# Routing ahead of expert 0, zeros under the scattered sums, and another order of the last experts

## The chip, the cores and the metric

The kernel runs on one core of a Trainium2 chip. A time is device microseconds of one execution, and the figure that counts is the median of a few executions on the same chip. TensorE (PE, with PEld for its weight loads), VectorE (DVE), ScalarE (ACT) and GpSimd (POOL) each work through their own instructions in order; SyncE (SP) does little else than issue transfers. POOL issues some transfers too.

## What is computed

One decoder layer for 512 tokens of width 1024: a token mixer (two kinds of attention, gated and projected), a layer norm, then a mixture of 32 experts of which each token takes 4, and a second layer norm. Cut to what matters here:

```python
x = layer_norm(ALPHA * x + token_mixer(x), ln1_g, ln1_b)          # y below
logits = x @ router_w + router_b
top_val, top_idx = top_k(logits, 4); gates = softmax(top_val)
# for each expert e, over the tokens that chose it:
#   g = min(x @ w_gate[e] + b_gate[e], 7); u = clip(x @ w_up[e] + b_up[e], -7, 7)
#   ffn[token] += gate * ((g * sigmoid(1.702 * g) * (u + 1)) @ w_down[e] + b_down[e])
out = layer_norm(ALPHA * x + ffn, ln2_g, ln2_b)                     # ALPHA = 2 ** 0.25
```

All is float32. One expert's three weight matrices are 12 MiB, all of them 384 MiB, and every expert's weights are read once.

## The kernel before, in words

**Front.** x and the projection weights are loaded in 1 MiB chunks through a ring of SBUF tiles, split into a high and a low part by ACT and DVE, and multiplied on PE. The very first chunk comes in four pieces, each with its two rows of x (`first_chunk`). Attention, gates and output projection follow. At the end of this part `norm_tile(t)` makes the normed rows y of 128 tokens (t = 0 to 3) in the tiles `r_tiles[t]`, POOL stores them to `y_dram`, PE turns them into `yT`, and after every second tile `route_places` multiplies them with the router's weights (PE, tile `pl`), takes the top 4 and gives each token its place in its experts' lists (`pos1`). ACT computes the norm's square root there, and later the exponentials of the softmax; between the two it loads another function table.

**Experts.** Two fixed experts (0 and 1) come first; the other 30 are ranked by their token counts on the chip (`rank_experts`), and the list `TURNS` says which rank is taken when. The first 18 in rank have two blocks of slots, A and B ("big"), the others one block ("small"). `slots` finds an expert's tokens with DVE compares and small PE products, and POOL gathers their rows from `y_dram` (tile `xg`). `ffn` then runs the expert: the rows are turned (`ptx`, `tx`), `pga` (and `pgb` for block B) collect gate and up, DVE and ACT make the hidden rows (`up`), PE turns them (`pth`, `th`), `pda` (and `pdb`) collect the result, ACT scales it by the routing weights (`sw`) to `ys`, and POOL adds those rows to `acc_dram` by a scattering transfer. `midway()` is code that stands between gate/up and down of expert i and prepares expert i + 2. In expert 0 it first calls `first_weights`: the ranking, the softmax weights (`route_weights`, result `gat`), the weights' split for experts 0 and 1 (`info`) and their products on PE (`late_weights`, tile `pw`), then ALPHA times y on ACT and four stores of it to `acc_dram`, with which the sums begin. Then the tiles of y are released, and two more ring tiles (`ring_d`) take their place.

**Weights.** SP issues the 384 chunks of expert weights in order into rings of 21 chunk tiles in all. A chunk's transfer waits until the chunk 21 before it has been used by PE (for a big expert by its block B too), and from expert 2 on the address needs the ranking (`order_i`).

**End.** `load_sums` reads the four tiles of `acc_dram`, the last expert's rows are added by a product with a 0/1 matrix (`psf`, read by DVE at L1014), and the second norm follows, tile by tile. A branch that would take further blocks of overfull experts stands between the loads and that product.

The order of the instructions on each engine is set by a scheduler from the program's dependences and priorities; only what follows `issue_after` is held behind a named instruction.

Of the kernel before, what the change touches and what calls it, by code (L numbers as in the profile page):

```python
# [19 lines left out]
P = 128  # L20
S = 512
# [15 lines left out]
def _turns():  # L37

    big, small = list(range(FIXED, BIG)), list(range(BIG, NE))
    turns, n, early = list(range(FIXED)), NE - FIXED - 1, NE - BIG - 1  # L40
    for i in range(n):
        some = small if len(small) > 1 and (NE - BIG - len(small)) * n <= i * early + n // 2 + 2 else big
        turns.append(some.pop(0))
    return turns + small


TURNS = _turns()
# [10 lines left out]
def decoder_kernel(tc, d):  # L58
# [3 lines left out]
    def mm(out, lhsT, rhs, start, stop, pos=None):  # L62
        if pos is None:
            T.matmul(out, lhsT, rhs, start=start, stop=stop)  # L64
        else:
            T.matmul(out, lhsT, rhs, start=start, stop=stop, tile_position=pos)  # L66
# [67 lines left out]
    ps = psO.tile([P, S], F32, name="ps_warm", tag="o")  # L134
    for n in range(8):
        mm(ps, warm[:, :P], warm, True, True)

    oT_h = [p_out.tile([P, S], F32R, name=f"oTh{c}") for c in range(10)]
    oT_l = [p_out.tile([P, S], F32R, name=f"oTl{c}") for c in range(10)]
# [370 lines left out]

    ring_c = tc.alloc_tile_pool(name="ring_c", bufs=RING[3], side="right")
    rings.append(ring_c)
    dpool = tc.alloc_tile_pool(name="dp", bufs=1, space=DRAM)
    y_dram = dpool.tile([S + P, D], F32, name="y_dram")
    acc_dram = dpool.tile([S + P, D], F32, name="acc_dram")

    mo1 = tc.alloc_tile_pool(name="mo1", bufs=1, side="right")
    p_y = tc.alloc_tile_pool(name="p_y", bufs=1, side="right")
    p_ln = tc.alloc_tile_pool(name="p_ln", bufs=1, side="left")
# [55 lines left out]
    def norm_tile(t):  # L575

        y = r_tiles[t]
        yT = yT_tiles[t % 2]
        sums = p_ln.tile([P, 2], F32, name=f"sums{t}", tag="sums", bufs=2)
        with tc.high_priority():  # L580
            for n in range(2):
                cs = slice(n * 512, (n + 1) * 512)
                V.scalar_tensor_tensor(y[:, cs], y[:, cs], ALPHA, mix[t][n], op0=ALU.mult, op1=ALU.add,
                                       accum_out=sums[:, n:n + 1])
            sq = yT[0].rearrange("p k c -> p (k c)").bitcast(BF16)
            nmu, rs = norm_stats(y, sums, sq, p_ln, f"a{t}")
        for n in range(2):
            cs = slice(n * 512, (n + 1) * 512)
            V.scalar_tensor_tensor(y[:, cs], y[:, cs], nmu, g1[:, cs], op0=ALU.add, op1=ALU.mult)
        for n in range(2):  # L590
            cs = slice(n * 512, (n + 1) * 512)
            V.scalar_tensor_tensor(y[:, cs], y[:, cs], rs, b1[:, cs], op0=ALU.mult, op1=ALU.add)
        G.dma_start(y_dram[t * P:(t + 1) * P, :], y)
        if t == 0:
            G.dma_start(y_dram[S:, :], y)
        for n in range(2):
            pt = psT.tile([P, S], F32, name=f"yTp{t}{n}", tag="t")
            for k in range(4):
                T.transpose(pt[:, k * P:(k + 1) * P], y[:, (4 * n + k) * P:(4 * n + k + 1) * P], ident)
            last["yT"] = A.copy(yT[n], pt.rearrange("p (k c) -> p k c", k=4))  # L600
        return yT
# [10 lines left out]
        V.tensor_tensor(oh, C[:, None, None, C_IOTA:C_IOTA + NE].broadcast_to([P, 2, 4, NE]),  # L612
                        if8[:, :, 0:4, None].broadcast_to([P, 2, 4, NE]), op=ALU.is_equal)

    def route_places(tp, yTs):

        t0 = 2 * tp
        pl = psA.tile([P, S], F32, name=f"pl{tp}", tag="acc")
        for tt in range(2):
            for k in range(KT):  # L620
                mm(pl[:, tt * NE:(tt + 1) * NE], yTs[tt][k // 4][:, k % 4, :], rw[:, k, :], k == 0, k == KT - 1)
        lg = small([2, NE], "lg", tp, pool=p_ln)
        V.tensor_tensor(lg, pl[:, :2 * NE].rearrange("p (t e) -> p t e", t=2),
                        rb[:, None, :].broadcast_to([P, 2, NE]), op=ALU.add)
        v8, i8, if8 = small([2, 8], "v8", tp), small([2, 8], "i8", tp, U32), small([2, 8], "if8", tp)
        for tt in range(2):
            V.max(v8[:, tt, :], lg[:, tt, :])
            V.max_index(i8[:, tt, :], v8[:, tt, :], lg[:, tt, :])
        V.tensor_copy(if8, i8)
        oh = small([2, 4, NE], "oh", tp, pool=p_ln)  # L630
        choose(oh, if8)
        mask = small([2, NE], "mask", tp, pool=p_ln)
        V.tensor_reduce(mask, oh.rearrange("p t k e -> p t e k"), axis=AX.X, op=ALU.add)
        V.tensor_copy(maskb[:, t0:t0 + 2, :], mask)
        pp = psA.tile([P, S], F32, name=f"pp{tp}", tag="acc")
        for tt in range(2):
            for u in range(t0 + tt + 1):
                mm(pp[:, tt * NE:(tt + 1) * NE], ubf if u == t0 + tt else obf, maskb[:, u, :], u == 0, u == t0 + tt)
        last["place"] = V.scalar_tensor_tensor(
            pos1[:, t0:t0 + 2, :], pp[:, :2 * NE].rearrange("p (t e) -> p t e", t=2), 1.0, mask,  # L640
            op0=ALU.add, op1=ALU.mult)
        return v8, if8

    def route_weights(tp, v8, if8):

        t0 = 2 * tp
        nmx, se, g4 = small([2], "nmx", tp), small([2], "se", tp), small([2, 4], "g4", tp)
        oh = scratch(f"weights{tp}", 8 * NE).rearrange("p (t k e) -> p t k e", t=2, k=4)
        choose(oh, if8)
        V.tensor_scalar(nmx, v8[:, :, 0], -1.0, None, op0=ALU.mult)  # L650
        for tt in range(2):
            A.activation(g4[:, tt, :], v8[:, tt, 0:4], AF.Exp, bias=nmx[:, tt:tt + 1], accum_out=se[:, tt:tt + 1])
        V.reciprocal(se, se)
        V.tensor_tensor(g4, g4, se[:, :, None].broadcast_to([P, 2, 4]), op=ALU.mult)
        V.tensor_tensor(oh, oh, g4[:, :, :, None].broadcast_to([P, 2, 4, NE]), op=ALU.mult)
        V.tensor_reduce(gat[:, t0:t0 + 2, :], oh.rearrange("p t k e -> p t e k"), axis=AX.X, op=ALU.add)
# [23 lines left out]
    for t in range(NT):  # L680
        mix_step(t, 4, first)
    late += w_out_splits(3)
    yTs, picks = [], []
    for t in range(NT):
        for n in range(2):
            for k in range(5, KT):
                mix_step(t, k, late[k - 5], (n,))
        yTs.append(norm_tile(t))
        if t % 2:
            picks.append(route_places(t // 2, yTs[-2:]))  # L690
    pc = psA.tile([P, S], F32, name="pc", tag="acc")
    for t in range(NT):
        mm(pc[:, :NE], obf, maskb[:, t, :], t == 0, t == NT - 1)
# [195 lines left out]
        V.tensor_reduce(order, table, axis=AX.X, op=ALU.add)  # L889
        V.tensor_copy(order_i, order[0:1])  # L890

    def first_weights():
        rank_experts()
        for tp in range(2):
            route_weights(tp, *picks[tp])
        for e in range(FIXED):
            sws[e] = late_weights(e, states[e], info_of(e, gat[:, :, e], mo1), psX, "t")
        for t in range(NT):
            A.mul(r_tiles[t], r_tiles[t], ALPHA)
            G.dma_start(acc_dram[t * P:(t + 1) * P, :], r_tiles[t])  # L900
        p_y.release()
        rings.append(tc.alloc_tile_pool(name="ring_d", bufs=RING[4], side="right", reuse_waits="tile"))

    def expert(i):
        def midway():
            if i == 0:
                first_weights()
            if i + 2 < NE:
                r = TURNS[i + 2]
                one = mo1.tile([P, NE], F32, name=f"one{i + 2}", tag="one", bufs=2)  # L910
                V.tensor_scalar(one, rank, float(r), None, op0=ALU.is_equal)
                place, weight = picked_columns(i + 2, one)
                states[i + 2], sws[i + 2] = all_slots(i + 2, 2 if r < BIG else 1, place[:, :, None],
                                                      order[:96, r:r + 1], weight, psX, "t")

        def next_rows():
            if i + 1 < NE:
                xts[i + 1] = rows_of_x(states[i + 1], i + 1)

        if i < FIXED:  # L920
            src = d["w_exp"][i]
        else:
            er = nc.values_load(order_i[:, TURNS[i]:TURNS[i] + 1], engines=[mybir.EngineType.SP], min_val=0,
                                max_val=NE - 1)
            src = d["w_exp"][bass.ds(er, 1)][0]
        return ffn(i, lambda c: load_expert(src[c], f"we{i}_{c}_"), states[i], lambda: sws[i], xts.pop(i), midway,
                   next_rows)
# [4 lines left out]
        add_rows(expert(i), states[i])  # L932

    ys_last, = expert(NE - 1)
    free = free_tiles(4)
    goes = free[0][:, :S]
    to = mo.tile([P, 1], F32, name="to")
    to_t = mo.tile([P, NT], F32, name="to_t")
# [5 lines left out]
    ln2 = free[1].rearrange("p (n c) -> p n c", n=2)  # L944
    nc.sync.dma_start(ln2[:, 0, :], d["ln2_g"].partition_broadcast(P))
    nc.sync.dma_start(ln2[:, 1, :], d["ln2_b"].partition_broadcast(P))
    sums = [t.rearrange("p (n c) -> p n c", n=2) for t in free[2:]]
    r_last = [sums[t // 2][:, t % 2, :] for t in range(NT)]

    def load_sums():  # L950
        for t in range(NT):
            nc.sync.dma_start(r_last[t], acc_dram[t * P:(t + 1) * P, :])

    load_sums()


# [172 lines left out]
```

## Time and profile before

| | |
|---|---|
| three runs | 1579.11, 1581.71, 1582.24 us (median 1581.71) |
| profiled execution | 1580.91 us, its span 1579.0 us |
| PE busy | 1472.5 us, 93% of the span |
| DVE, ACT, POOL busy | 463.5, 323.8, 154.4 us |
| moved by transfers | 475.27 MB, mean 301 GB/s |

The span is cut into 40 slices of about 39.5 us in the page's second part; each digit is the busy share of an engine, or of the 16 transfer engines, in tenths. A timeline row gives start, length, engine, line, operation, out<-in, how many instructions are merged in it, and in brackets how long the engine stood idle before it and what ended that. A row of waits gives a total, how many times, and the longest.

### The profile page before, as it was taken

How to read it: one execution, taken by the hardware profiler on the slowest of the kernel's cores; microseconds unless marked ns; L12 is line 12 of the kernel's file. 1: busy time of each engine (PE TensorE's matmuls, PEld its weight loads, DVE VectorE, ACT ScalarE, POOL GpSimd, SP SyncE). 2: the span in 40 equal slices, each digit the busy share in tenths (PEclk: the TensorE clock that was granted, in tenths of full speed). 3: DMA queues.
4: the chain of work that ended last, by engine and by line, in shares of the span. 5: the costliest groups of instructions: out<-in, count | busy, mean ns of one | idle time of the engine just before them, and what ended most of it. 6: DMA issues, size and time to landing. Idle time of an engine off the chain costs nothing. (4 is left out here: it accounts for less than half of the span.)

```text
span 1579.0 us, 24838 instructions
## 1 busy us (share of the span) xinstructions
PE 1472.5 (93%) x10022; PEld 794.1 (50%) x10022; DVE 463.5 (29%) x1344; ACT 323.8 (21%) x699; POOL 154.4 (10%) x121
## 2 busy tenths in 40 slices
PE   9999999999997799999998989988989998988993
PEld 6988767788885244353433335332433343332431
DVE  3134577764434331211221112111211111210114
ACT  4233466533323001011101001100101000100003
POOL 0000000000001011111111111111111010111102
PEclk9999999999996889999999999999999999999996
DMA  6202111333487399999999999999999999999992
GB/s 257 78 30 73 35 44 39 139 108 103 164 329 290 141 354 402 411 407 403 407 410 403 411 409 409 407 404 410 406 412 402 408 405 406 409 409 401 411 384 109
DMA packets 84758, 475.27 MB, mean 301 GB/s; under 512 B 10272, under 2 KB 12832, under 8 KB 39200
## 3 DMA queue, kind: packets, MB, share of 16 engines
q1 hardware_dynamic: 72864, 447.68, 70.2%
q0 software_dynamic: 11776, 25.96, 6.2%
q8 instruction: 81, 1.33, 0.3%
q14 instruction: 37, 0.30, 0.1%
HBM read 456.30 MB, written 17.30 MB: 300 GB/s over the span
## 5 line engine op out<-in xcount | busy, mean ns | idle before, releaser
L828 DVE TENSOR_SCALAR pga<-pga 128x512 f32<-128x512 f32 x32 | 22.4, 700 | 414.9 <-PE pga L800 414.9
L792 POOL DMA_INDIRECT acc_dram<-ys,ix x49 | 78.0, 1592 | 402.5 <-ACT ys L843 147.3
L728 POOL DMA_INDIRECT xg<-y_dram,ix x50 | 61.2, 1224 | 490.5 <-issue 364.1
L830 DVE TENSOR_SCALAR up<-pga 128x512 f32<-128x512 f32 x32 | 22.1, 692 | 230.8 <-PE pga L800 230.8
L784 ACT COPY th<-pth 128x512 f32<-128x512 f32 (+1 forms) x50 | 25.3, 506 | 296.5 <-PE pm L64 248.2
L117 DVE TENSOR_TENSOR wlin<-win,whin 128x1024 fp32r<-128x1024 f32 x42 | 51.3, 1225 | 117.5 <-ACT whin L116 112.0
L829 ACT ACTIVATE pga<-pga 128x512 f32<-128x512 f32 x32 | 18.6, 582 | 255.2 <-DVE pga L828 255.2
L843 ACT ACTIVATE ys<-pda,sw 128x512 f32<-128x512 f32 x32 | 22.0, 688 | 237.3 <-PE pda L800 218.6
L116 ACT CAST whin<-win 128x1024 fp32r<-128x1024 f32 x42 | 44.1, 1050 | 64.1 <-PE psk L64 15.3
L64 PE MATMUL psg<-xh,wlin 128*128 128x512 f32 x128 | 50.2, 392 | 0.0
L64 PE MATMUL psg<-xh,whin 128*128 128x512 f32 x128 | 50.1, 391 | 0.0
L64 PE MATMUL psg<-xl,whin 128*128 128x512 f32 x128 | 49.9, 390 | 0.0
L784 ACT COPY tx<-ptx 128x512 f32<-128x512 f32 (+1 forms) x50 | 24.4, 516 | 89.5 <-PE ptx L782 89.5
L800 PE MATMUL pga<-we_h,tx 128*64 128x512 f32 x152 | 41.4, 598 | 0.8 <-DMA we_h<-in_w_exp_dram 0.8
L800 PE MATMUL pga<-we_l,tx 128*64 128x512 f32 x152 | 41.2, 597 | 1.0 <-DMA we_l<-in_w_exp_dram 1.0
L537 POOL MEMSET obf<- 128x128 bf16 x1 | 0.2, 205 | 416.4 <-DVE merged L505 416.4
L828 DVE TENSOR_SCALAR pgb<-pgb 128x256 f32<-128x256 f32 x18 | 7.8, 433 | 103.9 <-PE pgb L800 103.9
L64 PE MATMUL mx<-whwo,merged 128*128 128x512 f32 x128 | 38.1, 400 | 0.0
L64 PE MATMUL psv<-wlin,xh 128*128 128x256 f32 x96 | 34.4, 358 | 0.0
L64 PE MATMUL psv<-whin,xl 128*128 128x256 f32 x96 | 34.4, 358 | 0.0
L64 PE MATMUL psv<-whin,xh 128*128 128x256 f32 x96 | 34.4, 358 | 0.0
L782 PEld LDWEIGHTS pth<-C,up 128*128 128x128 f32 x164 | 17.1, 141 | 31.6 <-issue 21.2
(1316 smaller groups left out, 2985.1 us busy)
## 6 DMA issues: line engine op xcount, KB each, us to landing
we_h<-in_w_exp_dram SPq DMA_DIRECT2D x54, 512.0 KB, 16.5
we_l<-in_w_exp_dram SPq DMA_DIRECT2D x54, 512.0 KB, 16.1
win<-in_w_in_dram SPq DMA_DIRECT2D x21, 1024.0 KB, 4.9
wpj<-in_w_proj_dram SPq DMA_DIRECT2D x8, 640.0 KB, 3.9
wo<-in_w_out_dram SPq DMA_DIRECT2D x4, 1024.0 KB, 4.9
y_dram<-r POOLq DMA_DIRECT2D x5, 512.0 KB, 5.8
x<-in_xT_dram SPq DMA_DIRECT2D x4, 512.0 KB, 6.6
r<-in_x_dram SPq DMA_DIRECT2D x4, 512.0 KB, 6.7
```

The source lines that it names most:

```text
L64: T.matmul(out, lhsT, rhs, start=start, stop=stop)
L116: A.copy(wh[:, :n], src)
L117: V.tensor_tensor(wl[:, :n], src, wh[:, :n], op=ALU.subtract)
L728: G.indirect_dma_start(out=x, out_offset=None, in_=table, in_offset=bass.IndirectOffsetOnAxis(ap=ix[:, 0:1], axis=0))
L782: T.transpose(pt[:, b * P:(b + 1) * P], src[:, b * P:(b + 1) * P], ident)
L784: A.copy(t, pt.rearrange("p (b h s) -> p b h s", b=tiles, h=pieces))
L792: G.indirect_dma_start(out=acc, out_offset=bass.IndirectOffsetOnAxis(ap=state[0][n][1][:, 0:1], axis=0), in_=ys[n], in_offset=None, comput ...
L800: last["mm"] = T.matmul(out[m * h:m * h + m, :], lhsT, rhs[:, h * w:(h + 1) * w], start=start, stop=stop, tile_position=(0, m * h), skip_g ...
L828: V.tensor_scalar(gt, gt, 7.0, None, op0=ALU.min)
L829: A.activation(gt, gt, AF.Gelu_apprx_sigmoid)
L830: V.tensor_scalar(h, up, 7.0, -7.0, op0=ALU.min, op1=ALU.max)
L843: A.mul(y, pd[n], sw()[n])
```

## The change

Four things are altered. The sums in `acc_dram` begin as zeros, written at the outset by 16 POOL transfers from the zeroed tile `warm`; the tile `y_dram` is declared there too. The rows of ALPHA times y are no longer stored there: at the end y is read back from `y_dram` into two more ring tiles, and DVE adds ALPHA times it to each loaded sum. The ranking, the routing weights and the split `info` of experts 0 and 1 stand ahead of expert 0; only the products `late_weights` stay in `midway`. The router's products are written tile by tile instead of for two tiles at once. And `TURNS` ends with three small experts: before, F F s s B B s B s B s B s B B s B s B s B s B B s B s B s B B s (F fixed, B big, s small); now F F s s B s B B s B B s B B s B s B B s B B s B B s B s B s s s.

```diff
@@ _turns
-    turns, n, early = list(range(FIXED)), NE - FIXED - 1, NE - BIG - 1
-    for i in range(n):
-        some = small if len(small) > 1 and (NE - BIG - len(small)) * n <= i * early + n // 2 + 2 else big
-        turns.append(some.pop(0))
-    return turns + small
+    turns = list(range(FIXED)) + small[:2]
+    middle, end = small[2:-3], small[-3:]
+    for i, r in enumerate(big):
+        turns += middle[i * len(middle) // len(big):(i + 1) * len(middle) // len(big)] + [r]
+    return turns + end
@@ at the start, after the warm-up products
+    for t in range(NT):
+        for n in range(4):
+            G.dma_start(acc_dram[t * P:(t + 1) * P, n * 256:(n + 1) * 256], warm.bitcast(F32))
@@ routing
+    def logits(pl, t, yT):
+        for k in range(KT):
+            mm(pl[:, t % 2 * NE:(t % 2 + 1) * NE], yT[k // 4][:, k % 4, :], rw[:, k, :], k == 0, k == KT - 1)
...
-        yTs.append(norm_tile(t))
+        yT = norm_tile(t)
+        if t % 2 == 0:
+            pl = psA.tile([P, S], F32, name=f"pl{t}", tag="acc")
+        logits(pl, t, yT)
...
-    def first_weights():
-        rank_experts()
-        for tp in range(2):
-            route_weights(tp, *picks[tp])
-        for e in range(FIXED):
-            sws[e] = late_weights(e, states[e], info_of(e, gat[:, :, e], mo1), psX, "t")
-        for t in range(NT):
-            A.mul(r_tiles[t], r_tiles[t], ALPHA)
-            G.dma_start(acc_dram[t * P:(t + 1) * P, :], r_tiles[t])
-        p_y.release()
-        rings.append(tc.alloc_tile_pool(name="ring_d", bufs=RING[4], side="right", reuse_waits="tile"))
+    rank_experts()
+    for tp in range(2):
+        route_weights(tp, *picks[tp])
+    first_info = [info_of(e, gat[:, :, e], mo1) for e in range(FIXED)]
+    p_y.release()
+    rings.append(tc.alloc_tile_pool(name="ring_d", bufs=RING[4], side="right", reuse_waits="tile"))
@@ midway of expert 0
-                first_weights()
+                for e in range(FIXED):
+                    sws[e] = late_weights(e, states[e], first_info[e], psX, "t")
@@ the end
-    free = free_tiles(4)
+    free = free_tiles(6)
...
+    for t in range(NT):
+        nc.sync.dma_start(y_last[t], y_dram[t * P:(t + 1) * P, :])
 
     def load_sums():
         for t in range(NT):
             nc.sync.dma_start(r_last[t], acc_dram[t * P:(t + 1) * P, :])
+            V.scalar_tensor_tensor(r_last[t], y_last[t], ALPHA, r_last[t], op0=ALU.mult, op1=ALU.add)
```

How the order of the instructions moves shows at three places. The first is DVE in expert 0. Before, the six instructions that make its hidden rows (`pga`, `up`, `pgb`) stand ahead of the ranking (`table`, `rank`):

```order
L828 TENSOR_SCALAR pga_3999<-pga_3999 128x512
L830 TENSOR_SCALAR up_4040<-pga_4000 128x512
L831 SCALAR_TENSOR_TENSOR up_4040<-up_4040,pga_3999 128x512
L828 TENSOR_SCALAR pgb_4002<-pgb_4002 128x256
L830 TENSOR_SCALAR up_4117<-pgb_4002 128x256
L831 SCALAR_TENSOR_TENSOR up_4117<-up_4117,pgb_4002 128x256
L885 TENSOR_TENSOR table<-key 128x1024
L886 TENSOR_REDUCE rank<-table 128x32
```

Now the ranking follows the last index of the first gathers (`ix`); the first instruction of expert 0 on `pga` comes only 32 rows behind the first of these on `table`:

```order
L731 SCALAR_TENSOR_TENSOR ix_3961<-pm_3955,dst_3960 128x1
L656 RECIPROCAL se_4022<-se_4022 128x2
L891 TENSOR_TENSOR table<-key 128x1024
L657 TENSOR_TENSOR g_4023<-g_4023,se_4022 128x8
L979 MEMSET blk 128x1
L892 TENSOR_REDUCE rank<-table 128x32
L893 TENSOR_TENSOR table<-rank,C 128x1024
```

The ranking, six rows behind the first clamp of `pga` before, now stands 32 rows ahead of it, and routing with it. The second place is PE behind the turn of expert 0's hidden rows (`pth`). Before, the down product `pda` comes first, and the small products `pw` only behind it:

```order
L800 MATMUL pda_4001<-we_8__4254,th_4127 64x512 x4
L800 MATMUL pda_4001<-we_9__4256,th_4127 64x512 x4
L800 MATMUL pda_4001<-we_10__4258,th_4127 64x512 x4
L800 MATMUL pda_4001<-we_11__4260,th_4127 64x512 x4
L800 LDWEIGHTS sel_3922
L800 MATMUL pdb_4003<-bh,sel_3922 32x256
...
L64 LDWEIGHTS oh_3896
L64 MATMUL pw_4171<-info_4163,oh_3896 128x3
```

Now `pw` stands ahead of `pda`, and the products of expert 2's places (`pm`) inside it:

```order
L788 MATMUL pth_4192<-C,up_4110 128x128 x4
L64 LDWEIGHTS oh_3912
L64 MATMUL pw_4199<-info_4033,oh_3912 128x3
...
L806 MATMUL pda_4071<-we_8__4262,th_4197 64x512 x4
L806 MATMUL pda_4071<-we_9__4264,th_4197 64x512 x3
L64 LDWEIGHTS oh_4245
L64 MATMUL pm_4247<-info_4237,oh_4245 128x5
```

The router's products on PE keep their places, although they are written in another order. The third place is the end on DVE, ahead of the branch. The four adds of y stand there, behind the last instruction that prepares the 0/1 matrix (`free_11366`), and the register load `total` and the branch behind them:

```order
L945 TENSOR_SCALAR free_11366<-C,to_t 128x128 x4
L958 SCALAR_TENSOR_TENSOR free_11370<-free_11368,free_11370 128x1024 x2
L958 SCALAR_TENSOR_TENSOR free_11371<-free_11369,free_11371 128x1024 x2
L980 TENSOR_LOAD total
L981 COMPARE_AND_BRANCH
```

All four adds are new there; before, the load of `total` followed the matrix at once.

## Rows read from the trace of the kernel before

**Rows 1.** The page, part 2: PE's busy tenths and what moved, in 40 slices.
```profile
PE   9999999999997799999998989988989998988993
...
GB/s 257 78 30 73 35 44 39 139 108 103 164 329 290 141 354 402 411 407 403 407 410 403 411 409 409 407 404 410 406 412 402 408 405 406 409 409 401 411 384 109
```

**Rows 2.** Windows of 4 us: busy PE, PEld, DVE, ACT, POOL; clock, transfers' share, GB/s.
```profile
520.00:524.00 4.00, 4.00 (x22) 1.26 (x18) 0.00 (x0) 0.00 (x0) 0.00 (x0) 1.00 0.00 0
...
536.00:540.00 4.00, 4.00 (x20) 1.15 (x16) 0.00 (x0) 0.00 (x0) 0.00 (x0) 1.00 0.01 2
540.00:544.00 4.00, 0.66 (x7) 0.30 (x6) 3.78 (x6) 0.00 (x0) 0.00 (x0) 0.95 0.00 0
544.00:548.00 4.00, 0.00 (x0) 0.00 (x0) 4.00 (x11) 0.00 (x0) 0.00 (x0) 0.50 0.00 0
```

**Rows 3.** Waits of SP, the weights' issuer, from 440 to 620 us.
```profile
SPq L80 <- PE pgb L800: 28.6, 7, 14.5
SPq L80 <- DMA acc_dram<-r: 25.9, 2, 16.1
...
SPq L923 <- DVE sel L733: 19.5, 1, 19.5
```

**Rows 4.** Timeline of PE through expert 0's down product, and through expert 1's.
```profile
538.22 1.89 PE L800 MATMUL pda<-we__4260,th 128*64 128x512 f32 x8
...
551.46 0.75 PE L64 MATMUL pw<-info,oh 128*128 128x3 bf16 x16 [10.79 <-DVE info L665]
...
562.03 1.94 PE L800 MATMUL pga<-we__4339,tx 128*64 128x512 f32 x8
...
589.75 1.89 PE L800 MATMUL pda<-we__4532,th 128*64 128x512 f32 x8
...
596.51 1.94 PE L800 MATMUL pga<-we__4616,tx 128*64 128x512 f32 x8
```

**Rows 5.** Timeline of DVE: expert 0's first clamp, ranking's first, routing's last instruction.
```profile
517.70 0.70 DVE L828 TENSOR_SCALAR pga<-pga 128x512 f32<-128x512 f32 x1 [14.21 <-PE pga L800]
...
540.15 1.23 DVE L885 TENSOR_TENSOR table<-key 128x1024 bf16<-128x1024 f32 x1 [6.00 <-PE pda L800]
...
551.23 0.24 DVE L665 CAST info<-rest 128x4 bf16<-128x4 f32 x2
```

**Rows 6.** The gathers: POOL's second issue, PE's wait, landings (480 to 620 us).
```profile
502.09 1.00 POOL L728 DMA_INDIRECT xg<-y_dram,ix  x1 [0.30 <-DVE blk L973]
...
507.72 0.69 PE L782 MATMUL ptx<-C,xg 128*128 128x128 f32 x2 [1.08 <-DMA xg<-y_dram,ix]
...
DMA to landing us min/median/max: 4.7/7.7/8.5
```

**Rows 7.** Timeline of ACT: a copy behind the last norm's root; a table load.
```profile
486.90 0.59 ACT L600 COPY yTb<-yTp 128x512 f32<-128x512 f32 x1 [0.77 <-PE yTp L599]
...
498.53 1.28 ACT L652 ACT_TABLE_LOAD   x1
```

**Rows 8.** Start: x's last piece on ACT; POOL's queue, 600 to 1500 us (packets, MB, share).
```profile
12.17 1.05 ACT L179 CAST xh<-x 128x1024 fp32r<-128x1024 f32 x1 [0.36 <-DMA x<-in_xT_dram]
...
q0 software_dynamic: 9282, 18.84, 8.5%
```

**Rows 9.** End: last chunk's issue, transfers (KB each, landing), the last product, sums, first L1014.
```profile
1518.22 0.33 SPq L80 DMA_DIRECT2D we__11336<-in_w_exp_dram  x1
...
we__11336<-in_w_exp_dram SPq DMA_DIRECT2D x1, 1024.0 KB, 21.7
free<-acc_dram SPq DMA_DIRECT2D x4, 512.0 KB, 8.0
...
1536.67 1.75 SPq L952 DMA_DIRECT2D free<-acc_dram  x4
...
1543.77 1.89 PE L800 MATMUL pda<-we__11336,th 128*64 128x512 f32 x8
...
1549.37 0.69 DVE L1014 SCALAR_TENSOR_TENSOR free<-psf,free 128x512 f32<-128x512 f32 x1 [11.46 <-PE psf L66]
```

More of the change, by code (lines that the diff above doesn't have):

```diff
@@ L136, in decoder_kernel @@
         mm(ps, warm[:, :P], warm, True, True)
+    dpool = tc.alloc_tile_pool(name="dp", bufs=1, space=DRAM)
+    y_dram = dpool.tile([S + P, D], F32, name="y_dram")
+    acc_dram = dpool.tile([S + P, D], F32, name="acc_dram")
+    for t in range(NT):
+        for n in range(4):
+            G.dma_start(acc_dram[t * P:(t + 1) * P, n * 256:(n + 1) * 256], warm.bitcast(F32))
     oT_h = [p_out.tile([P, S], F32R, name=f"oTh{c}") for c in range(10)]
@@ L512, in decoder_kernel @@
     rings.append(ring_c)
-    dpool = tc.alloc_tile_pool(name="dp", bufs=1, space=DRAM)
-    y_dram = dpool.tile([S + P, D], F32, name="y_dram")
-    acc_dram = dpool.tile([S + P, D], F32, name="acc_dram")
     mo1 = tc.alloc_tile_pool(name="mo1", bufs=1, side="right")
@@ L613, in choose, with route_places @@
                         if8[:, :, 0:4, None].broadcast_to([P, 2, 4, NE]), op=ALU.is_equal)
-    def route_places(tp, yTs):
+    def logits(pl, t, yT):
+        for k in range(KT):
+            mm(pl[:, t % 2 * NE:(t % 2 + 1) * NE], yT[k // 4][:, k % 4, :], rw[:, k, :], k == 0, k == KT - 1)
+    def route_places(tp, pl):
         t0 = 2 * tp
[L618 to L621, printed above, removed]
         lg = small([2, NE], "lg", tp, pool=p_ln)
@@ L682, in decoder_kernel @@
     late += w_out_splits(3)
-    yTs, picks = [], []
+    picks = []
     for t in range(NT):
@@ L687, in decoder_kernel @@
                 mix_step(t, k, late[k - 5], (n,))
-        yTs.append(norm_tile(t))
+        yT = norm_tile(t)
+        if t % 2 == 0:
+            pl = psA.tile([P, S], F32, name=f"pl{t}", tag="acc")
+        logits(pl, t, yT)
         if t % 2:
-            picks.append(route_places(t // 2, yTs[-2:]))
+            picks.append(route_places(t // 2, pl))
     pc = psA.tile([P, S], F32, name="pc", tag="acc")
@@ L946, in decoder_kernel @@
     nc.sync.dma_start(ln2[:, 1, :], d["ln2_b"].partition_broadcast(P))
-    sums = [t.rearrange("p (n c) -> p n c", n=2) for t in free[2:]]
-    r_last = [sums[t // 2][:, t % 2, :] for t in range(NT)]
+    tiles = [t.rearrange("p (n c) -> p n c", n=2) for t in free[2:]]
+    y_last = [tiles[t // 2][:, t % 2, :] for t in range(NT)]
+    r_last = [tiles[2 + t // 2][:, t % 2, :] for t in range(NT)]
+    for t in range(NT):
+        nc.sync.dma_start(y_last[t], y_dram[t * P:(t + 1) * P, :])
     def load_sums():
```

## The prediction, made blind

> **What bounds the kernel now.** I read the page first: PE is busy for 93% of the span, but the line of GB/s splits the run in two [rows 1]. In slices 1 to 12 PE is full and the transfers mostly are not. From slice 16 to 38 they move some 401 to 412 GB/s in every slice, and PE's digits fall below 9 here and there. So the first third is paced by PE, the rest by the bytes of the experts' weights, and the end of that stream sets the end of the run. A change pays in the second part only if it lets the stream fill earlier, takes bytes from it, or shortens what follows its last chunk.
>
> Next I looked at the seam, from 500 to 600 us, in windows. The transfers stand still at 520 to 524 and again from 536 to 548 [rows 2], with most of the weights still to come. The waits of the issuing engine say why: it waited 28.6 us for PE to give up chunk tiles, 19.5 us for the ranking that names expert 2's address, and 25.9 us for the stores of the starting sums to let go of the y tiles [rows 3]. PE itself stands still there too: behind expert 0's down product it waits 10.79 us for DVE's `info`, and its granted clock falls from the 2.4 to the 1.2 GHz level while it does nothing [rows 2, 4]. DVE's timeline closes the chain: it idled 14.21 us before expert 0's first clamp, began the ranking only at 540.15, after PE's down product (the table shares a buffer with the turned hidden rows that this product reads), and needed until 551.5 for ranking and routing [rows 5]. Its inputs were there at about 502, when the second gather is issued [rows 6], and it was done 49 us later, with everybody waiting for it.
>
> **Part by part.** I count in the profiled span of 1579.0 us.
>
> *Routing ahead of expert 0.* From the start of the last `pda` group to expert 1's first gate product PE took 562.03 - 538.22 = 23.81 us. Behind expert 1, where no routing stands, the same stretch took 596.51 - 589.75 = 6.76 us [rows 4]. The difference is 17.05. Of it the 0.75 us of `pw` remains, now ahead of the down product, and two more row turns than expert 1 had cost some 0.3, an estimate from the 0.69 of such a pair [rows 4, 6]. That leaves -16.0. Does DVE's block fit where it is put? It took 551.47 - 540.15 = 11.3 us; begun at about 502 it ends near 514, ahead of the first clamp at 517.70 [rows 5]. Behind it are queued only clamps, and PE needs their result later still, at the turn of the hidden rows. From here on the weights' tiles come free 16 us earlier, and since the transfers are slack until then, the stream fills 16 us earlier. The ends of this term: -13 if a part of the wait returns at `pm` inside the down product, -17 at best.
>
> *No stores of ALPHA y.* 2.1 MB leave the seam. They shared the transfer engines with the first gathers: the second was issued at 502.09 and PE could use it at 507.72, 5.6 us, where the quickest gather of this stretch took 4.7 [rows 6]. With the queue nearly empty I take 3.6, so -2.0, with 0 and -2.7 as ends. The y tiles are let go earlier as well, but that chunk was not late for PE; nothing.
>
> *Softmax next to the norms.* In the new order ACT takes the exponentials of tiles 0 and 1 between the norms of tiles 2 and 3, so the square root's table must be loaded again before the last norm: 1.28 us [rows 7]. ACT has 0.77 us of air before its next copy [rows 7], PE waits for that copy, and two small DVE instructions are in the way: +0.8, between 0 and 1.8. Writing the router's products tile by tile moves nothing on PE.
>
> *Zeros at the outset.* 16 transfers of 128 KB, 2048 packets of 1 KB, now run while x and the first weights come in. There PE is paced by the loads: the last piece of x is converted as it lands at 12.17 [rows 8], and from there PE is full to slice 12 [rows 1], so any delay is paid. The bounds: 0 if the zeros find gaps; and if a small packet takes as long as POOL's packets did in the full stream, 8.5% of 16 engines times 900 us over 9282 packets = 132 ns each [rows 8], then 2048 of them take 16.9 engine-averaged us, of which the loads of the first 12 us, one packet for one, feel about half: 8.4. By bytes at 408 GB/s [rows 1] all zeros cost 5.1, half of them 2.6. Zero packets are smaller than the rows they are taken from, so bytes are nearer: +2.5.
>
> The Trainium skill (DMA: Bandwidth & Descriptors, "Measured") gives 32% efficiency at 64 KB a transfer and 78% at 1 MB; by it sixteen of 128 KB would cost around 10 us as an estimate rather than 5.1, and the start about 5 rather than 2.5. No run here has such writes alone yet.
>
> *y read back, sums completed at the end.* SP's order puts the y loads behind the last chunk and ahead of the sums. The last chunk, issued at 1518.22, landed 21.7 later at 1539.9; the sums were issued until 1538.4 and landed 8.0 later, near 1546 [rows 9]. Another 2.1 MB in front of them is 5.1 us, less about 1 of a gap that the sums' late issue left there. Then come four adds of 128x1024, of which three run while the next sum lands and the last, 1.23 by the 128x1024 of [rows 5], does not: the last sum is ready near 1551.5 on the old clock, where L1014 began at 1549.37 [rows 9]. +2.1, between -2 (loads hidden) and +5.
>
> *Three small experts last.* At the end PE used the last chunk 3.9 us after it had landed (1543.77 against 1539.9) [rows 9], since two big experts stood ahead; behind small ones it will use it on landing. That would be worth up to 3.9, but the sums are later than PE now, so here it is worth 0. In the middle, PE's demand for big-big-small stays under the stream's time, so nothing moves there.
>
> The sum: -16.0 - 2.0 + 0.8 + 2.5 + 2.1 = -12.6. Span 1566.4; the execution was 1.9 longer than its span, and the median of the runs 0.8 above that execution: 1569.1. I say **1569**.
>
> **The rivals.**
> *The zeros hold the start.* At 8.4 instead of 2.5, with the later products of the first chunk also bunched, the median would be 1575. For it: loads and zeros meet just where PE waits for loads. Against it: POOL must issue each transfer by itself, which spreads them. The page named above points the same way.
>
> *The wait only moves.* If ranking, start of the ring and `pm` still hold PE for half of the 16 us, inside expert 0 or at expert 1, the median is 1577; if nearly all of it returns, 1582. Against it: the block ends 3 us ahead of the first clamp. For it: DVE's small instructions for expert 2 are now mixed in between the clamps.
>
> *The stream does not start earlier (slower).* The one mechanism is that bytes, not tiles, limit the seam: then the 18 us vanish, and the start, ACT's table and the end remain: 1579.0 + 0.8 + 2.5 + 2.1 + 2.7 = 1587. It decides if the transfers are still full or the first chunk that waits for expert 1's block B is still issued near 577. Against it stand the windows with a share of 0.00 and 0.01 [rows 2].
>
> **How the numbers follow.** Forecast 0.72, zeros hold the start 0.12, half of the wait returns 0.04 and nearly all 0.05, the stream does not start earlier 0.07. The forecast's own range is 1564 to 1574 from the ends of its terms, which do not all fall to one side; the second rival and half of the third bring it to 1577. Two in ten or fewer lie outside 1563 to 1577. A measurement of this kernel can tell about 0.2%, 3.2 us, from no change. Faster by more: 0.72 + 0.12 + 0.04 = 0.88, and I keep 0.86; same 0.06; slower 0.08.
>
> **What would show it.** PE's wait for `info` is gone and expert 1's first gate product follows the last `pda` group by under 8 us. Transfers run without a hole from about 526 to 550 and stay full from about 562. The last weight chunk lands near 1525 to 1528. At the start, x's last piece is converted 2 to 3 us later than 12.17. At the end DVE, not PE, begins last: L1020 follows the fourth add. I am wrong if the transfers are full but the last chunk lands where it did, if PE stands behind DVE in expert 0, or if x comes over 6 us late.

## The result, and the profile after

The changed kernel takes 1571.42 us (median of 6 runs, 1569.70 to 1572.44), the kernel before 1580.41 beside it (median of 6): a ratio of 0.9944, 95% interval 0.9929 to 0.9959. It is faster, by 9 us where I said 12.6. The profiled execution has a span of 1570.6 against 1579.0 us: 8.4 less.

The page's second part shows the same two halves as [rows 1]; what is new is the first slice, with more bytes moved and PE a tenth lower, and slice 14, where the stall was:

```profile
PE   8999999999996999999999899989999899889872
...
GB/s 311 59 50 54 54 44 18 137 133 90 131 344 299 220 362 410 408 404 409 405 405 408 408 408 407 405 409 407 409 411 400 412 400 407 412 393 412 410 404 89
```

The seam in windows of 4 us (busy PE, PEld, DVE, ACT, POOL; clock, transfers' share, GB/s), to be laid beside [rows 2]:

```profile
516.00:520.00 4.00, 4.00 (x20) 1.26 (x18) 0.62 (x2) 0.00 (x0) 0.00 (x0) 1.00 0.00 0
...
528.00:532.00 4.00, 4.00 (x84) 2.19 (x76) 0.00 (x0) 0.00 (x0) 0.00 (x0) 1.00 0.85 299
...
540.00:544.00 4.00, 4.00 (x22) 1.68 (x18) 3.32 (x18) 0.72 (x2) 0.95 (x1) 1.00 1.00 420
544.00:548.00 4.00, 4.00 (x73) 2.07 (x73) 0.25 (x1) 1.00 (x3) 1.63 (x1) 1.00 1.02 418
...
560.00:564.00 4.00, 4.00 (x54) 1.70 (x54) 1.38 (x2) 0.00 (x0) 0.00 (x0) 1.00 0.49 147
```

PE is full and at the 2.4 GHz level where it stood still before. The transfers are full from 532 to 560, dip to a share of 0.49 once more, and are full again from 568 on. PE's timeline through expert 0's down product, against [rows 4], has `pw` ahead of `pda` without a wait, and expert 1's first gate product 7.2 us behind the last group of `pda`, not 23.8:

```profile
533.86 0.35 PE L64 MATMUL pw<-info,oh 128*128 128x3 bf16 x8
...
540.94 2.30 PE L806 MATMUL pda<-we__4268,th 128*64 128x512 f32 x7
...
548.12 1.89 PE L806 MATMUL pga<-we__4347,tx 128*64 128x512 f32 x8
```

The start of the run and its last expert's end are worse than before. At the start POOL's zeros go out among the loads, and x's last piece is converted at 15.81, not 12.17 [rows 8] (timelines of POOL and ACT):

```profile
2.55 4.54 POOL L143 DMA_DIRECT2D acc_dram<-warm  x8 [1.70 <-ACT warm L133]
...
11.87 2.80 POOL L143 DMA_DIRECT2D acc_dram<-warm  x5 [0.25 <-DMA acc_dram<-warm]
```
```profile
15.81 1.05 ACT L186 CAST xh<-x 128x1024 fp32r<-128x1024 f32 x1 [1.65 <-DMA x<-in_xT_dram]
```

At the end the last chunk is issued 12.9 us earlier than in [rows 9], but DVE's four additions wait for the sums, and PE and ACT stand behind them at the branch (`DVEq L981` in their brackets); the four products `psf` then run at the 1.2 GHz level, 2.08 us where they took 1.13 before. Timelines of SP, PE, DVE and ACT:

```profile
1505.35 0.33 SPq L80 DMA_DIRECT2D we__11344<-in_w_exp_dram  x1
...
1512.75 7.74 SPq L953 DMA_DIRECT2D free<-y_dram  x4
1522.73 5.43 SPq L957 DMA_DIRECT2D free<-acc_dram  x4
```
```profile
1527.02 1.89 PE L806 MATMUL pda<-we__11344,th 128*64 128x512 f32 x8
1540.85 2.08 PE L66 MATMUL psf<-ys,free 64*128 64x512 f32 x4 [11.94 <-DVEq L981]
```
```profile
1535.02 2.44 DVE L958 SCALAR_TENSOR_TENSOR free<-free,free 128x1024 f32<-128x1024 f32 x2 [15.55 <-SPq L981]
1538.19 2.45 DVE L958 SCALAR_TENSOR_TENSOR free<-free,free 128x1024 f32<-128x1024 f32 x2 [0.73 <-SPq L981]
1542.93 0.69 DVE L1020 SCALAR_TENSOR_TENSOR free<-psf,free 128x512 f32<-128x512 f32 x1 [2.28 <-PE psf L66]
```
```profile
1540.78 1.28 ACT L1036 ACT_TABLE_LOAD   x1 [11.14 <-DVEq L981]
```

Marks on PE's and DVE's timelines cut both spans into stretches, and their differences add up to the 8.4:

| stretch | before | after | difference |
|---|---|---|---|
| start to the first `psv` | 41.76 | 43.24 | +1.5 |
| to the last product of `mx` | 440.7 | 441.6 | +0.9 |
| router, to `pp` of the last two tiles | 14.7 | 15.1 | +0.4 |
| gathers, to expert 0's first gate product | 11.15 | 11.01 | -0.1 |
| expert 0's gate and up, to its `pda` | 23.9 | 23.1 | -0.8 |
| to expert 1's `pda` (the stall was here) | 51.6 | 35.7 | -15.8 |
| to the last chunk's `pda` | 959.9 | 957.2 | -2.8 |
| to the first L1014, now L1020 | 5.6 | 15.9 | +10.3 |
| to the end of the span | 29.6 | 27.7 | -2.0 |

The second stretch is scatter: in the fourteen profiles the last product of `mx` began between 477.8 and 486.7, with a granted clock of 0.95 to 1.00 over the first 160 us, so I compare stretches, and totals only by their intervals. The stretches too come from one profile of each kernel: the third took 13.2 to 15.2 us in the fourteen, the fifth 22.6 to 24.2, so their +0.4 and -0.8 say little. The -2.8 ahead of the last chunk's `pda` is the new order's: with the old order in the changed kernel (below) that stretch took 961.8.

### The profile page after: what moved, and what is told of

The parts are those of the page before. It is cut to its first block, busy times and chain, and to the rows that moved or that the text cites. A ratio compares the mean times of both kernels' runs of the same rounds, so it can differ in the third digit from the quotient of the medians.

```text
span 1570.6 us, 24882 instructions
## 1 busy us (share of the span) xinstructions
PE 1469.7 (94%) x10022; PEld 808.3 (51%) x10022; DVE 467.0 (30%) x1348; ACT 322.3 (21%) x697; POOL 161.7 (10%) x133
## 5 line engine op out<-in xcount | busy, mean ns | idle before, releaser
L739 DVE TENSOR_SCALAR sel<-C,order 96x64 bf16<-96x64 f32 x30 | 7.4, 247 | 92.3 <-PE pdb L806 92.3
```

## The experiments

Each ratio is against the kernel before, run on the same chip beside it.

| kernel | median us | ratio, 95% |
|---|---|---|
| the change | 1571.42 | 0.9944 (0.9929 to 0.9959) |
| routing alone | 1561.60 | 0.9891 (0.9873 to 0.9908) |
| routing and order | 1564.80 | 0.9910 (0.9895 to 0.9924) |
| change, zeros late | 1568.65 | 0.9939 (0.9920 to 0.9957) |
| change, additions behind the branch | 1573.61 | 0.9963 (0.9949 to 0.9977) |
| change, old order | 1572.50 | 0.9953 (0.9936 to 0.9971) |
| routing and order, clock held (16) | 1564.16 | 0.9912 (0.9897 to 0.9928) |
| change, y tiles kept | 1568.74 | 0.9940 (0.9926 to 0.9954) |
| change without y at the end | 1565.04 | 0.9908 (0.9892 to 0.9923) |
| routing alone, DRAM tiles early | 1562.15 | 0.9900 (0.9879 to 0.9921) |
| routing and order, clock held (8) | 1564.28 | 0.9908 (0.9888 to 0.9928) |
| before, with zeros | 1576.46 | 0.9992 (0.9981 to 1.0004) |
| routing alone, zeros late | 1559.49 | 0.9891 (0.9872 to 0.9909) |

**Routing alone.**

```diff
+    rank_experts()
+    for tp in range(2):
+        route_weights(tp, *picks[tp])
+    first_info = [info_of(e, gat[:, :, e], mo1) for e in range(FIXED)]
+    alpha = rt.tile([P, 1], F32, name="alpha")
+    V.tensor_scalar(alpha, order[:, 0:1], 0.0, ALPHA, op0=ALU.mult, op1=ALU.add)
     def first_weights():
-        rank_experts()
...
-            A.mul(r_tiles[t], r_tiles[t], ALPHA)
+            A.mul(r_tiles[t], r_tiles[t], alpha)
```

> The kernel before with one part of the change alone: ranking, routing weights and info ahead of expert 0. The sums still begin as ALPHA times y, stored in the seam (their factor now comes out of the ranking, so that the stores stay behind the first gathers), no zeros, nothing read back, old order of the experts. My theory (the stall at info held the whole stream of weights): the last chunk is issued about 15 us earlier than 1518.22 and the span goes from 1579.0 to 1563 to 1565, median about 1565, so this part alone is worth more than the whole change (1571.4). Rival 1, the seam's gain needs the y tiles free early and no stores there: the stream gains 8 or less and the median stays at 1572 or above. Rival 2, the end eats what the stream gains whatever stands there: the last chunk is 15 earlier, but the span shrinks by no more than 9.

0.9891: this one part is worth more than the whole change; the intervals do not touch. The stretch from expert 0's `pda` to expert 1's is 35.7 us as in the change, and the last chunk is issued at 1496.39. Both rivals fall, and the expected 1565 was 3 us too cautious. The rest of the change therefore costs some 8 us, and the runs below look for them. The gathers were a surprise. PE waited 2.1 us for `xg`, not 4.2, and its first gate product stands 8.9 us behind `pp` instead of 11.0:

```profile
492.99 0.19 PE L64 MATMUL pp<-maskb,ubf 128*128 128x32 bf16 x1 [1.99 <-DVE maskb L634]
...
500.11 1.76 PE L782 MATMUL ptx<-C,xg 128*128 128x128 f32 x6 [2.12 <-DMA xg<-y_dram,ix]
501.90 2.65 PE L800 MATMUL pga<-we__4035,tx 128*64 128x512 f32 x8
```

**Routing and order.** The same, with the changed `_turns`.

> As the run with routing alone, and the new order of the experts with three small ones last. By my prediction the order is worth nothing, because the sums land later than PE finishes: within 1 us of the run with routing alone. Rival: PE, and the 0/1 product behind it, not the sums, begin the end; then the last chunk is used as it lands and this run is 2 to 4 us shorter than the one with routing alone.

0.9910 against 0.9891: the intervals overlap; the order gains nothing here, and rather loses. The stretches say why. PE begins the last chunk's `pda` 3.5 us earlier (1042.7 us behind `mx`, where it was 1046.2; the gathers are alike), then gives it back: the first addition of `psf` follows that `pda` by 7.4 us, not 5.1, and the rest takes 30.0 us, not 27.2. With small experts last PE waits for chunks (from 1450 to 1500 us it is busy 42.1 us, not 50.0), it begins `psf` 3.5 us after its last product, not 2.1, and its clock is then at the 1.2 GHz level. PE's timeline with routing alone, then with the order too (`PEq` in a bracket is PE's own sequencer, here at the branch):

```profile
1524.02 1.88 PE L800 MATMUL pda<-we__11338,th 128*64 128x512 f32 x8
1528.01 1.13 PE L66 MATMUL psf<-ys,free 64*128 64x512 f32 x4 [2.11 <-PEq L980]
```
```profile
1525.02 1.89 PE L800 MATMUL pda<-we__11338,th 128*64 128x512 f32 x8
1530.38 2.08 PE L66 MATMUL psf<-ys,free 64*128 64x512 f32 x4 [3.47 <-PEq L980]
```

**Clock held.** To test that, small products fill PE between the last `pda` and the branch.

```diff
     ys_last, = expert(NE - 1)
+    with tc.issue_after(last["mm"].ins):
+        hold = psD.tile([P, S], F32, name="hold", tag="b")
+        for n in range(16):
+            mm(hold, bh[:, :P], bh[:, :S], True, True)
```

> The run with routing and the new order, plus sixteen small bfloat16 products into an unused bank between the last expert's down product and the branch, so that PE does not stand still there. Theory (the clock of the last products is what the three small experts lose): the first psf takes about 1.13 us instead of 2.08, DVE waits about 0.3 instead of 1.3 us for each later pair, and the run is 2 to 4 us shorter than 1564.8, at or below the run with routing alone. Rival 1, the branch is passed late for another reason (PE passed it 3.5 us after its last product there, 2.1 with the old order): psf begins as late as before or later, by up to 2 us, and the run does not gain.

The clock is the cause of the longer rest: `psf` took 1.13, DVE waited 0.36 us for the next pair, and from the first L1023 to the end it is 27.2 us, not 30.0. But PE began `psf` no earlier, 6.4 us behind the start of the last `pda` where it was 5.4:

```profile
1526.15 3.63 PE L64 MATMUL hold<-bh 96*128 96x512 bf16 x16
1530.72 1.13 PE L66 MATMUL psf<-ys,free 64*128 64x512 f32 x4 [0.94 <-PEq L984]
```

The 2.8 us show in the profile, which is of the fastest of its six executions (1561.20, the others 1562.99 to 1566.27); the medians (1564.16, 1564.80) don't tell the two apart, so the expected 2 to 4 us do not show there.

That the new order brings the low clock is not shown. In the six kernels without zeros this rest took 27.2 us where the clock stayed up through all of `psf` (routing alone, the same with the DRAM tiles early, and the sixteen products) and 29.6 to 30.1 where it fell (the kernel before, routing and order, and the eight products below). The kernel before has the old order, and its clock fell behind the first four `psf`. In the run with the additions behind the branch, further down, PE waited 3.41 us ahead of `psf`, as long as here, and `psf` took 1.13. With eight products (and the DRAM tiles early):

> The run with held clock, with eight instead of sixteen filling products and the DRAM tiles declared at the outset. If PE's passing of the branch is what is late, not the filling products, psf begins 6 us behind the start of the last pda whatever stands between, as with none and with sixteen; its four take 1.13 us if eight are enough to hold the clock. Median 1562 to 1564.5. If the sixteen were in the way, psf begins up to 1.7 us earlier.

`psf` came 7.0 us behind the start of the last `pda` and took 2.08 again. The sixteen were not in the way.

The traces show something else that goes with PE's passing of the branch. The list of DMA queues has a queue 8 of kind "instruction", with 81 packets of 16 KB in a run. In each of the ten profiles in which PE did not stand behind DVE's additions there, a packet of it starts 2.8 to 2.9 us ahead of `psf`: at 1525.19 for 1528.01 with routing alone, 1527.54 for 1530.38 with the order, 1527.93 for 1530.72 with sixteen products, 1526.49 for 1529.34 with eight. So PE seems to wait there for its next instructions. Against the start of the last `pda` that packet lies anywhere from 0.9 to 4.2 us behind it, and later with the new order: `psf` then begins 5.3 to 7.0 us behind that start in five profiles, with the old order 3.7 to 4.6 in the other five. No run moves the packet alone, and why it starts when it does is open.

**Zeros late.**

```diff
     for g in range(3):
         dil_values(g)
+    V.tensor_scalar(warm[:, 1:2], vdil[2][:, 3, 0:1], 0.0, None, op0=ALU.mult)
+    for t in range(NT):
+        for n in range(4):
+            G.dma_start(acc_dram[t * P:(t + 1) * P, n * 256:(n + 1) * 256], warm.bitcast(F32))
```

> The changed kernel with its sixteen transfers of zeros held back until the values of the dilated attention exist (one DVE write of zero times such a value into the zeroed tile), at a place where the transfers are nearly idle. Theory: the zeros at the outset cost what x's last piece and PE lost there, so x's last piece is converted near 12.2 us again instead of 15.81, the last product of mx comes 2.4 us earlier, and the span is 2 to 3 us below 1570.6, median about 1569. Rival, the start was late for another reason (the loads' own scatter between executions): no change.

x's last piece came at 12.15 and the first `psv` at 41.97, where the change had 15.81 and 43.24: the zeros cost the start 1.3 to 1.5 us. In the total (0.9939 against 0.9944) this does not stand out.

**Before, with zeros.** Only the DRAM tiles and the sixteen transfers are taken over into the kernel before.

> The kernel before with the DRAM tiles and the sixteen transfers of zeros at the outset and nothing else (the stores of ALPHA times y overwrite them). My theory from the changed kernel: x's last piece is converted at 15.6 to 15.8 instead of 12.17, the first product psv begins 1.3 to 1.5 us later than 41.76, and that is the whole price: median 1.5 us above the kernel before, or, if the zeros are also what shortens the end by 2.3 us, 0.8 us below it. By my prediction: 2.5 us above. Rival, the zeros cost more later on the queue of POOL: over 4 us above.

0.9992: no difference. x's last piece came at 15.91 and `psv` at 43.31, as in the change, and the span ended 3.7 us behind the last store's issue, not 5.7: the same transfers that cost 1.5 at the start give back 2 at the very end. My +2.5 is refuted as a price of the zeros in the whole run, and the rival falls too.

**Additions behind the branch.**

```diff
-            V.scalar_tensor_tensor(r_last[t], y_last[t], ALPHA, r_last[t], op0=ALU.mult, op1=ALU.add)
@@ last_rows
         r = r_last[t]
+        V.scalar_tensor_tensor(r, y_last[t], ALPHA, r, op0=ALU.mult, op1=ALU.add)
```

> The changed kernel with the four additions of ALPHA times y placed behind the branch, at each tile's last step, instead of ahead of it. Theory (PE and ACT cannot pass the branch before DVE, and DVE stands at the additions for the sums' transfers): psf and the load of the square root's table run at about 1530 to 1532, while the sums are still under way, the first L1020 follows the third addition at about 1539.5 instead of 1542.93, and the span is 3 to 6 us shorter. Rival, the landing of the sums alone sets the end and PE merely waits along: within 1.5 us of the changed kernel.

0.9963, not better than the change: the theory falls. PE and ACT did pass the branch early, and `psf` ran at 1532; but the first three additions now began only at 1538.72 and the first L1020 came at 1542.13, where the change had 1542.93:

```profile
1532.14 1.13 PE L66 MATMUL psf<-ys,free 64*128 64x512 f32 x4 [3.41 <-PEq L980]
```
```profile
1538.72 3.50 DVE L1012 SCALAR_TENSOR_TENSOR free<-free,free 128x1024 f32<-128x1024 f32 x3 [19.43 <-SPq L980]
1542.13 0.68 DVE L1020 SCALAR_TENSOR_TENSOR free<-psf,free 128x512 f32<-128x512 f32 x1
```

The scheduler had put three additions together ahead of the first L1020, so this is no clean test of additions tile by tile. It does show that freeing PE and ACT from the branch gains nothing while the sums come this late.

**Without y at the end.** The four loads of y and the four additions are taken out of the change.

> The changed kernel without the four loads of y at the end and without the four additions: ALPHA times y is left out of the result, nothing else. It prices what stands between the last chunk and the first L1020. By my prediction this costs 2.1 us. Theory from the traces: the first L1020 stood 15.9 us behind the start of the last pda in the changed kernel and 7.4 in the run with routing and the new order; the price is 4 to 7 us: median 1565 to 1567. Rival, what is late is PE's passing of the branch and not the sums: under 2.5 us.

0.9908 against 0.9944, and 1079.8 us from `mx` to the end where the change took 1085.7: reading y back and adding it costs about 6 us. The sums were issued from 1515.11, 7.4 us behind the last chunk where the change needed 17.4, and the first addition of `psf` followed the last `pda` by 9.0 us instead of 15.9. Then PE set the pace: it began `psf` 5.1 us after its last product, and at the 1.2 GHz level. The instruction packet ahead of `psf` started only at 1531.77, so 6 us may be less than y costs:

```profile
1527.66 1.89 PE L806 MATMUL pda<-we__11344,th 128*64 128x512 f32 x8
1534.62 2.08 PE L66 MATMUL psf<-ys,free 64*128 64x512 f32 x4 [5.07 <-PEq L977]
```

**Change, old order.** `_turns` as before.

> The changed kernel with the old order of the experts (one small expert last). By my prediction the order is worth nothing here: median within 1.5 us of 1571.4. Theory after the runs with routing alone and with routing and the new order (1561.6 against 1564.8): with small experts last PE waits for every chunk and stands still before the 0/1 product, which then runs at the 1.2 GHz level (2.08 us for four, against 1.13); with the old order PE starts its last pda some 3 to 4 us later, and the sums are late anyway, so the order is worth 1.5 to 3.5 us against the change: median 1568 to 1570. Rival: with the sums this late, PE waits 10 us for the branch in either order, the clock is low in either, and the old order only makes PE later: 1571 to 1573.

0.9953 against 0.9944: the rival holds, no difference. PE's last `pda` came 4.7 us later (1534.27 - 572.44 from expert 1's `pda`, where the change had 1527.02 - 569.86), and the first L1020 stood 11.4 us behind it instead of 15.9: what PE loses or gains there, the sums take back. All four additions ran in one piece, so DVE waited for no later sum, and `psf` ran at the 1.2 GHz level all the same:

```profile
1538.37 5.05 DVE L958 SCALAR_TENSOR_TENSOR free<-free,free 128x1024 f32<-128x1024 f32 x4 [11.47 <-SPq L981]
```
```profile
1543.62 2.08 PE L66 MATMUL psf<-ys,free 64*128 64x512 f32 x4 [7.48 <-DVEq L981]
```

**Change, y tiles kept.** Where routing alone had quick gathers and the change had not, SP's timeline of the change shows two chunks issued into tiles that y had just left, in front of the gathers:

```profile
489.10 0.35 SPq L80 DMA_DIRECT2D we__4367<-in_w_exp_dram  x1
499.70 0.33 SPq L80 DMA_DIRECT2D we__4534<-in_w_exp_dram  x1
527.46 0.34 SPq L80 DMA_DIRECT2D we__4536<-in_w_exp_dram  x1
```

The experiment holds the tiles until the ranking is done:

```diff
+    later = rt.tile([P, NT], F32, name="later")
+    for t in range(NT):
+        V.tensor_tensor(later[:, t:t + 1], r_tiles[t][:, 0:1], order[:, 0:1], op=ALU.mult)
     p_y.release()
```

> The changed kernel with four one-column DVE reads of the y tiles behind the ranking, so that the two chunk tiles that take their place come free only at about 511 instead of 489 and 500 us. Theory (the gathers' gain of my prediction is there, but two 1 MiB chunks issued into the freed tiles take it away): these two chunks go behind the gathers, PE waits about 2.1 instead of 4.2 us for xg, the first gate product follows the product pp by 8.9 instead of 11.0 us, and the span is about 2 us shorter, median 1569 to 1570. Rival, the gathers are slow for themselves here: no change.

The same two chunks went out at 509.32 and 509.87, PE waited 2.05 us for `xg` instead of 4.23, and the gate product came 8.86 us behind `pp`. The collision is shown, and its price in that stretch is 2.1 us. In the total (0.9940 against 0.9944) it is inside the intervals. First the change, then this kernel:

```profile
509.24 1.54 PE L788 MATMUL ptx<-C,xg 128*128 128x128 f32 x6 [4.23 <-DMA xg<-y_dram,ix]
```
```profile
504.23 1.88 PE L788 MATMUL ptx<-C,xg 128*128 128x128 f32 x6 [2.05 <-DMA xg<-y_dram,ix]
```

**DRAM tiles early, and zeros that serve nothing.** Two runs on the end of the span.

> The run with routing alone, with the two DRAM tiles declared at the outset as in the changed kernel, nothing else. In the profiles so far the span ends 5.7 to 5.8 us behind the issue of the last store in the four kernels without zeros, and 3.4 to 3.6 in the six with them. If the place of the tiles does it, the span ends about 3.4 behind the last issue and the median is 2 us below 1561.6, near 1559.5. If not, this is a repetition of the run with routing alone: 1560.5 to 1562.5.

> Routing ahead of expert 0 with the sums still begun as ALPHA times y and the old order, plus sixteen transfers of zeros into the sums' tile in the idle stretch after the dilated values (they are overwritten and serve nothing else). In seven profiles with such transfers the span ends 3.4 to 3.7 us behind the last store's issue, in six without them 5.7 to 5.8. If the transfers themselves do that, this run ends 2 us earlier than the same kernel without them (1561.6 and 1562.15): median about 1560. If it was something else, 1561 to 1563. Either way x's last piece is converted near 12.2 us.

The place of the tiles does nothing: 1562.15, and 5.8 us behind the last issue again. With the transfers it is 3.6, so the transfers do it. SP's last stores without them (span 1556.2) and with them (span 1556.8):

```profile
1539.22 11.22 SPq L1034 DMA_DIRECT2D out_dram<-free  x4
```
```profile
1541.95 11.22 SPq L1038 DMA_DIRECT2D out_dram<-free  x4
```

In the total the kernels with and without them (0.9891 against 0.9891 and 0.9900) are not to be told apart. In the profiles the clock takes back what the end gives: with the transfers it fell behind the first four `psf`, and the rest took 27.9 us where it was 27.2. Routing alone, with or without them, is the best version I have.

## Why the prediction was right or wrong

**The bound and the stall** were read rightly. The first third is PE's, the rest the stream's; nobody waits for `info` any more; the stretch shrank by 15.8 where I had 16.0. The ranking and all of the routing but two small steps of `info` ran on DVE ahead of the first clamp (519.38), and those two ended at 520.6, long before `pw` at 533.86. None of the three rivals came.

**Gathers, -2.0.** The mechanism and the size were right where the transfers are nearly empty: -2.2 with routing alone, -2.3 with the y tiles kept. In the changed kernel it was -0.1. The step that failed is the one I costed at nothing, "the y tiles are let go earlier as well": it starts two 1 MiB chunks, and they take the room that the stores of y left.

**ACT's table, +0.8:** 0.4 between the two profiles, inside what that stretch scatters from kernel to kernel.

**Zeros, +2.5.** x came 3.6 us later, and PE's first `psv` 1.5. The bytes were nearer than the small packets, as I chose; for PE they were still too much by 1. By the estimate from the Trainium skill (DMA: Bandwidth & Descriptors, "Measured", a table of loads into SBUF) the start would have been about 5 later; the trace does not bear that out, with 3.6 at x and 1.5 on PE. That the end gets shorter by 2 was in no row that I had.

**y read back, +2.1,** is the term that was mis-sized most. Taking it out gains 6, which is outside the -2 to +5 that I gave. Two steps failed. I let three additions run under the landing of the sums; two did, and the fourth ended at 1540.64, which is 1553.5 on the old clock, 2.0 later than I had. And I took the product `psf` as ready; but the additions stand ahead of the branch, and PE began it only behind them, at half the clock: 2.3 more to the first L1020. The later pairs cost little more than they did: DVE waited 1.2 to 1.5 us for each, and 1.1 to 1.2 in the kernel before, whose clock had fallen by then too (the second pair, before and after):

```profile
1551.89 0.69 DVE L1014 SCALAR_TENSOR_TENSOR free<-psf,free 128x512 f32<-128x512 f32 x1 [0.96 <-PE psf L66]
1552.84 0.69 DVE L1014 SCALAR_TENSOR_TENSOR free<-psf,free 128x512 f32<-128x512 f32 x1 [0.25 <-PE psf L66]
```
```profile
1545.79 0.69 DVE L1020 SCALAR_TENSOR_TENSOR free<-psf,free 128x512 f32<-128x512 f32 x1 [1.30 <-PE psf L66]
```

How much of the 6 is the 2.1 MB in front of the sums and how much the additions is not separated: the runs show that the sums are issued 10 us sooner without y, and that moving the additions alone gains nothing.

**Order, 0.** Right, and for the reason given, that the sums are later than PE. With the sums early it still gained nothing, for one that I had not seen: PE reached the last chunk 3.5 us earlier, but began `psf` later behind it, as in every profile of the new order, and in that profile at the low clock, which is not shown to be the order's.

So of 12.6, the stall gave what I said; 1.9 of the gathers went to chunks that started early, and some 4 more than I counted went to y at the end. That 1571.4 still lies inside 1564 to 1574 is in part luck: the end of the span got 2 us shorter for a reason that I had not seen, and the start cost PE 1 less than I had.

## What to carry to other kernels

A tile that comes free earlier starts a transfer earlier: ask what that transfer will run beside before costing it at nothing. Work on one engine in front of a branch can hold the others there: PE stood 11.9 us and ACT 11.1 us behind DVE's additions. Bytes put in front of the last loads delay them, and little is left to hide it: the sums were issued 10 us later behind the last chunk. And a change of four parts should be taken apart: the one part that removed the stall was worth more alone than with the three that came with it.

## What the runs showed of the hardware that I had not expected

The span ended 5.7 to 5.8 us behind the issue of the last store in the six profiles without the transfers of zeros, and 3.4 to 3.7 in the eight with them, wherever in the run they stood. Why is open.

The first four products `psf` took 1.13 us at a granted clock of 1.00 and 2.08 at 0.50. What PE did just before does not sort the profiles: behind waits of 3.4 to 3.5 us it was 1.13 once and 2.08 once. All eight profiles with zeros had the low clock by the second pair, three of the six without; what decides it is open.

With no additions and no filling products ahead of the last branch, PE began `psf` 1.9 to 5.1 us after its last product, each time 2.8 to 2.9 us behind the start of a 16 KB packet of the instruction queue.
